# The up projection of a DiT layer: source order on all five engines, and the gated product through a PSUM bank

## The chip, the cores and the metric

The kernel runs on one core of a Trainium2 chip. The metric is the device time of one execution in microseconds (us). The kernel before took 873.97 us in the median of three runs (873.82, 873.97 and 875.6 us).

## The reference, cut to what matters

One layer of a diffusion transformer over 512 latent tokens of width 1024, in float32. A token mixer (retention and pooling) comes first; the part that the change touches is the second half, a gated MLP with a 3x3 depthwise convolution over the token grid (8 rows of 64) between the up projection and the activation:

```python
def _conv_ffn(u, rows, cols, w_up, conv_w, conv_b, w_down):
    h = (u @ w_up).reshape(B, rows, cols, 2 * D_FF)          # D_FF = 2816
    h = lax.conv_general_dilated(h, conv_w[:, :, None, :], (1, 1), 'SAME', ...) + conv_b
    a, b = jnp.split(h.reshape(B, L, 2 * D_FF), 2, axis=-1)
    return (jax.nn.gelu(a) * b) @ w_down
```

The result goes through a residual sum and a layer norm.

## The kernel before, in words

Every float32 product is three matmuls in the fp32r type. A helper (split, L86 to L91) casts an operand to a high part "hi" on ScalarE (ACT) and subtracts it from the operand on GpSimd (POOL) or VectorE (DVE), which gives the low part "lo" (the subtraction itself is L84). The helper mm3 (L94 to L96) then multiplies hi by hi, hi by lo and lo by hi into one PSUM bank.

The up stage is the loop over i at L1000. It takes 44 tiles of 128 features; tile i=2f is the "a" half and tile 2f+1 the "b" half of the gate pair f=0..21. Each tile is one PSUM bank of 128x512: 24 matmuls of 512 columns on TensorE (PE). For the first six tiles half of the columns are already done when the loop begins, and the loop does the other half. Then, for each tile:

- ACT writes the centre tap with the bias into an accumulator in SBUF (L1010) and two scaled copies (L1013);
- POOL adds these two copies, shifted, to the accumulator (L936), two taps;
- DVE does the other six taps (L938), each a multiply-add that reads the bank and the accumulator.

For an even tile ACT then applies gelu to the accumulator in place (gelu, L984). After the odd tile DVE multiplies the two accumulators (gated, L987). act_out makes the hi part of the product on ACT (L991) and the lo part on DVE (L84), both into the operand buffers of the down projection. up_prep(i) loads the weights of tile i (512 KB, issued on the SyncE queue, SP) and splits them: hi on ACT (L89, or L949 for every third tile), lo on POOL.

The down stage (L1044 on) multiplies the 22 products by w_down: 24 matmuls for each f, into eight banks that stay open. f=0, 1 and 2 are prepared by down_prep after the loop, f=3 (lo on DVE), f=4 (lo on POOL) and so on one ahead of their use. The layer norm at the end works on the finished banks.

What sets the order: `ordered(...)` names the engines whose instructions stay in the order of the source; the others are put in an order by a scheduler that goes by an estimate of when each instruction can start. In the up stage before, only SP keeps source order (`ORD3 = (E_SP,)`); PE, DVE, ACT and POOL are scheduled. Each engine then runs its own list strictly from the top, and an instruction that waits holds back those behind it on its engine.

Of the kernel before, what the change touches and what calls it, by code (L numbers as in the profile page):

```python
# [9 lines left out]
F32 = mybir.dt.float32  # L10
F32R = mybir.dt.float32r
AF = mybir.ActivationFunctionType
ALU = mybir.AluOpType

P = 128
D = 1024
# [4 lines left out]
NKT = D // P  # L21
NTB = SEQ // P
NFF = 2816 // P
# [9 lines left out]
E_PE, E_SP, E_DVE = mybir.EngineType.PE, mybir.EngineType.SP, mybir.EngineType.DVE  # L33
# [3 lines left out]
ORDS = (E_PE, E_SP, E_DVE, E_ACT, E_POOL)  # L37
# [1 line left out]
ORD1 = (E_SP,)  # L39
ORDB = (E_PE, E_SP)  # L40
ORD2 = (E_DVE, E_ACT, E_POOL)
ORD3 = (E_SP,)
ORDT = (E_SP,)


# [1 line left out]
def layer_kernel(ctx: ExitStack, tc: tile.TileContext, a: dict):  # L47
    nc = tc.nc
    act, dve, pool, pe, dma = nc.scalar, nc.vector, nc.gpsimd, nc.tensor, nc.sync
# [7 lines left out]
    def nm(s):  # L57
        count[0] += 1
        return f"{s}_{count[0]}"

    def slot(i, shape, dt=F32):
        return sb.tile(shape, dt, tag=f"S{i}", name=nm(f"S{i}"))

    def raw4(shape=(P, D)):
        return sb.tile(list(shape), F32, tag="raw", bufs=3, name=nm("raw"))
# [4 lines left out]
    def t2(shape=(P, SEQ), dt=F32):  # L70
        return sb.tile(list(shape), dt, tag="t2", bufs=8, name=nm("t2"))
# [8 lines left out]
    def bank():  # L80
        return ps_pool.tile([P, SEQ], F32, tag="ps", name=nm("ps"))

    def sub(eng, out, x, y):
        eng.tensor_tensor(out, x, y, ALU.subtract)  # L84

    def split(raw, shape, eng):  # L86
        hi = sb.tile(list(shape), F32R, tag="hi", bufs=2, name=nm("hi"))
        lo = sb.tile(list(shape), F32R, tag="lo", bufs=2, name=nm("lo"))
        act.copy(hi, raw)  # L89
        sub(eng, lo, raw, hi.bitcast(F32))  # L90
        return hi, lo  # L91
# [6 lines left out]
    def load(t, src):  # L98
        dma.dma_start(t, src)
        return t  # L100
# [41 lines left out]
    def alt():  # L142
        engs[0] += 1
        return dve if engs[0] % 2 else pool
# [6 lines left out]
    def ordered(*engines):  # L151
        if region[0] is not None:
            region[0].__exit__(None, None, None)
        region[0] = tc.manual_schedule(engines=set(engines)) if engines else None
        if engines:
            region[0].__enter__()
# [85 lines left out]
    def first_load(kt):  # L242
        for j in (kt, 8 + kt):
            load(ada_slot(j), a["wada"][j])
        return load(raw4((P, NF0)), a["w_first"][kt])
# [6 lines left out]
    def first_prep(kt, raw):  # L252
        w = split(raw, (P, NF0), pool)
        first_mod(kt)
        modulate(mod, kt, 8 + kt, xnT[:, kt, :], uh[:, kt, :], ul[:, kt, :], pool)
        return w
# [76 lines left out]
    ready = wh, wl  # L333
# [8 lines left out]
    for kt in range(NKT):  # L342
        wh, wl = ready
        if kt == 0:
# [7 lines left out]
            ready = split(first_load(1), (P, NF0), pool)  # L352
            first_mod(1)
            modulate(mod, 1, 9, xnT[:, 1, :], uh[:, 1, :], ul[:, 1, :], pool)
        elif kt + 1 < NKT:
            ready = first_prep(kt + 1, first_load(kt + 1))
# [534 lines left out]
    n_early = 6  # L891
# [27 lines left out]
    first_half(4)  # L919
    first_half(5)  # L920
    inner.__exit__(None, None, None)
    ordered(*ORD3)

    acts = [slot(s, [P, 8, SEQ], F32R) for s in (2, 7, 6, 5, 3, 0)]
    spare = [acts[i][:, 6:8, :].rearrange("p a b -> p (a b)") for i in (2, 5)]

    def grid(t):
        return t.rearrange("p (r c) -> p r c", r=ROWS)

    def tap(acc, src, w, dr, dc):  # L930
        r0, r1 = max(0, -dr), min(ROWS, ROWS - dr)
        c0, c1 = max(0, -dc), min(COLS, COLS - dc)
        o = grid(acc)[:, r0:r1, c0:c1]
        i = grid(src)[:, r0 + dr:r1 + dr, c0 + dc:c1 + dc]
        if w is None:
            pool.tensor_tensor(o, o, i, ALU.add)  # L936
        else:
            dve.scalar_tensor_tensor(o, i, w, o, ALU.mult, ALU.add)  # L938
# [3 lines left out]
    DVE_TAPS = (0, 2, 3, 5, 6, 8)  # L942
    prepped = {}
# [7 lines left out]
        return wh, wl  # L951

    def up_prep(i):
        if n_early <= i < 2 * NFF:
            raw = load(raw4((P, NKT, P)), a["w_up"][i])
            prepped[i] = (spare_split if i % 3 == 2 else split)(raw, (P, NKT, P), pool)

    def down_prep(f, eng):
        raw = load(raw4(), a["w_down"][f])
        return (split if f % 3 else spare_split)(raw, (P, D), eng)  # L960

    def up_mm(i):
        if i < n_early:
            half(i, 1)
            return early[i][0]
        wh, wl = prepped.pop(i)
        return feature_mm(wh, wl, NKT, u2h, u2l)

    srcs, accs = {}, {}

    def conv_taps(i, order):
        for n in order:
            tap(accs[i], srcs[i], convw[:, i, n:n + 1], *TAPS[n])
            yield

    def weave(*gens):
        gens = list(gens)
        while gens:
            for g in list(gens):
                if next(g, 0) == 0:  # L980
                    gens.remove(g)

    def gelu(f):
        act.activation(accs[2 * f], accs[2 * f], AF.Gelu_apprx_tanh)  # L984

    def gated(f):
        dve.tensor_tensor(accs[2 * f], accs[2 * f], accs[2 * f + 1], ALU.mult)  # L987

    def act_out(f):
        hi = acts[f // 8][:, f % 8, :]  # L990
        act.copy(hi, accs[2 * f])  # L991
        sub(dve, acts[3 + f // 8][:, f % 8, :], accs[2 * f], hi.bitcast(F32))

    def settle(i):
        if i >= 0 and i % 2 == 0:
            gelu(i // 2)
        elif i >= 0:
            gated(i // 2)

    for i in range(2 * NFF):  # L1000
        up_prep(i + 2)
        ps = up_mm(i)
        if i >= 2 * NFF - 2:
            src = t2()
            act.copy(src, ps)
        else:
            src = ps
        srcs[i] = src
        acc = accs[i] = t2()
        act.activation(acc, src, AF.Identity, bias=convb[:, i:i + 1], scale=convw[:, i, 4:5])  # L1010
        for n in POOL_TAPS:
            hs = t2()
            act.activation(hs, src, AF.Copy, scale=convw[:, i, n:n + 1])  # L1013
            tap(acc, hs, None, *TAPS[n])
        gens = [conv_taps(i, DVE_TAPS[:3])]
        if i:
            gens.insert(0, conv_taps(i - 1, DVE_TAPS[3:]))
        weave(*gens)
        settle(i - 1)
        if i >= 3 and i % 2 == 1:  # L1020
            act_out((i - 3) // 2)
    down0 = down_prep(0, pool)
    i = 2 * NFF - 1
    weave(conv_taps(i, DVE_TAPS[3:]))
    settle(i)
    act_out(NFF - 1)

    g2 = load(row(), gates[1:2, :].broadcast_to([P, D]))
    lng = load(row(), a["ln2_g"].broadcast_to([P, D]))
# [9 lines left out]
    def down(tb, f, wh, wl):  # L1039
        for hf, cs in enumerate(HALVES):  # L1040
            split_end = f == N_FRONT - 1 and hf == 1 and tb == NTB - 1
            down_mm(banks[tb][hf], tb, f, wh, wl, cs, f == 0, split_end)

    down1 = down_prep(1, dve)  # L1044
    for w, f in ((down0, 0), (down1, 1)):
        for tb in range(NTB - 1):
            down(tb, f, *w)
    ready = down_prep(2, pool)
    for w, f in ((down0, 0), (down1, 1)):
        down(NTB - 1, f, *w)  # L1050
    lasth = slot(1, [P, NFF - N_FRONT, D], F32R)
# [1 line left out]
    for f in range(2, N_FRONT):  # L1053
        w = ready
        if f + 1 < N_FRONT:
            ready = down_prep(f + 1, alt())
        for tb in range(NTB):
            down(tb, f, *w)
        if f >= N_FRONT - 8 and f % 2 == 0:
            i = (f - N_FRONT + 8) // 2  # L1060
            raw = load(raw4(), a["w_down"][N_FRONT + i])
# [143 lines left out]
```

## Time and profile before

| what | value |
|---|---|
| median of three runs | 873.97 us |
| the profiled execution | 874.79 us |
| its span, first to last instruction | 873.0 us |
| mean granted PE clock | 0.981 |
| busy: PE / DVE / ACT / POOL | 821.6 / 624.4 / 366.2 / 444.2 us |
| up stage (second halves of tiles 0 to 5, then 6 to 43) on PE | from about 500 to 726 us |

The busy times are sums over the whole span; the stretch from 500 to 760 us is the one to read here. In the rows below, a timeline row gives the start, the time from the first start to the last end, the engine, the line, the operation, the operands by name (t an accumulator or a scaled copy, ps a PSUM bank, S an operand buffer, hi and lo the parts of a weight, raw a loaded weight), and how many instructions it joins. The time in brackets is idle time ahead of the row and what ended it.

### The profile page before, as it was taken

The numbers are of one execution on the slowest core, as the hardware profiler recorded it, in microseconds if no ns is written. First come the engines' busy times: TensorE is split into PE (matmuls) and PEld (weight loads), VectorE is DVE, ScalarE is ACT, GpSimd is POOL, SyncE is SP. The second block draws the span as 40 slices with busy tenths as digits, with TensorE's granted clock in tenths as the row PEclk, the third lists the DMA queues.
The fourth block names the chain that finished last, engine by engine and source line by source line (L and its number), as shares of the span: only waits on it lengthen the run. The fifth ranks groups of instructions, "written<-read, shape, count | busy, mean of one in ns | idle before, by whom it ended". The sixth has DMA issues, their size and how long they took to land.

```text
span 873.0 us, 10556 instructions
## 1 busy us (share of the span) xinstructions
PE 821.6 (94%) x3865; PEld 678.5 (78%) x3865; DVE 624.4 (72%) x959; ACT 366.2 (42%) x575; POOL 444.2 (51%) x304
## 2 busy tenths in 40 slices
PE   6889989999999999998998899999999998799993
PEld 4667878778888888887787898888888776688883
DVE  7899996676267773346757769999999999612138
ACT  4434544121444343233335476666655565223200
POOL 4877411121543230113456878899888886212245
PEclk9999999999999999999999999999999999999997
DMA  9932466767221104344503312222222252224202
GB/s 352 345 105 94 127 207 218 236 226 216 72 73 49 50 1 145 100 154 163 196 1 121 121 50 84 86 96 99 96 97 95 75 169 83 87 97 144 73 1 96
DMA packets 33780, 106.94 MB, mean 122 GB/s; under 512 B 4528, under 2 KB 5312, under 8 KB 33728
## 3 DMA queue, kind: packets, MB, share of 16 engines
q1 hardware_dynamic: 33728, 106.27, 35.6%
q8 instruction: 30, 0.49, 0.2%
q14 instruction: 22, 0.18, 0.1%
HBM read 104.14 MB, written 2.11 MB: 122 GB/s over the span
## 4 chain that ended last, share of the span: by engine, by line
PE 40%; DVE 39%; POOL 8%; DMA 6%; issue 5%; ACT 2%; SPq 0%; DVEq 0%; POOLq 0%; ACTq 0%
DVE t L938 19%; PE ps L96 11%; PE ps L95 11%; PE ps L94 11%; DVE S L84 4%; DMA raw<-in_wada 4%; DVE t L987 3%; POOL lo L84 3%; DVE raw L203 2%; DVE lo L84 2%; PE ps L339 1%; POOL S L84 1%; POOL sm L123 1%; PE ps L608 1%; DVE sm L130 1%
## 5 line engine op out<-in xcount | busy, mean ns | idle before, releaser
L96 PE MATMUL ps<-S,lo 128*128 128x512 f32 (+1 forms) x544 | 212.2, 392 | 5.1 <-DVE lo L84 4.7
L94 PE MATMUL ps<-S,hi 128*128 128x512 f32 (+1 forms) x544 | 213.6, 393 | 2.7 <-ACT hi L89 2.7
L95 PE MATMUL ps<-S,hi 128*128 128x512 f32 (+1 forms) x544 | 212.5, 391 | 0.2 <-POOL S L84 0.2
L84 POOL TENSOR_TENSOR lo<-raw,hi 128x1024 fp32r<-128x1024 f32 (+1 forms) x53 | 134.0, 2530 | 107.2 <-ACT hi L89 105.3
L938 DVE SCALAR_TENSOR_TENSOR t<-ps,convw,t 128x441 f32<-128x441 f32 (+1 forms) x252 | 167.6, 693 | 15.8 <-POOL t L936 11.5
L89 ACT CAST hi<-raw 128x1024 fp32r<-128x1024 f32 (+1 forms) x98 | 98.9, 1009 | 168.2 <-PE ps L95 61.7
L96 PEld LDWEIGHTS ps<-S,lo 128*128 128x128 f32 x544 | 102.8, 189 | 29.8 <-DVE lo L84 6.8
L94 PEld LDWEIGHTS ps<-S,hi 128*128 128x128 f32 x544 | 103.6, 190 | 23.7 <-ACT hi L89 3.1
L936 POOL TENSOR_TENSOR t<-t,t 128x448 f32<-128x448 f32 x88 | 116.7, 1329 | 10.0 <-ACT t L1013 6.2
L95 PEld LDWEIGHTS ps<-S,hi 128*128 128x128 f32 x544 | 103.7, 191 | 21.3 <-POOL S L84 0.6
L95 PE MATMUL ps<-S,S 128*128 128x512 f32 (+1 forms) x308 | 113.8, 370 | 5.4 <-DVE S L84 5.0
L94 PE MATMUL ps<-S,S 128*128 128x512 f32 (+1 forms) x308 | 113.1, 369 | 3.6 <-DVE t L938 3.6
L96 PE MATMUL ps<-S,S 128*128 128x512 f32 (+1 forms) x308 | 113.8, 370 | 0.2 <-POOL S L84 0.2
L84 DVE TENSOR_TENSOR lo<-raw,hi 128x1024 fp32r<-128x1024 f32 (+1 forms) x47 | 61.4, 1307 | 53.0 <-ACT hi L89 53.0
L84 POOL TENSOR_TENSOR S<-raw,S 128x1024 fp32r<-128x1024 f32 x21 | 50.8, 2423 | 68.7 <-ACT S L735 44.5
L95 PE MATMUL ps<-lo,S 128*128 128x512 f32 x208 | 81.6, 392 | 0.7 <-DVE lo L84 0.6
L96 PE MATMUL ps<-hi,S 128*128 128x512 f32 x208 | 81.3, 391 | 0.0
L94 PE MATMUL ps<-hi,S 128*128 128x512 f32 x208 | 79.2, 392 | 0.0
L95 PEld LDWEIGHTS ps<-S,S 128*128 128x128 f32 x308 | 58.9, 191 | 15.6 <-DVE S L84 5.5
L94 PEld LDWEIGHTS ps<-S,S 128*128 128x128 f32 x308 | 58.6, 191 | 13.6 <-DVE t L938 4.0
L96 PEld LDWEIGHTS ps<-S,S 128*128 128x128 f32 x308 | 58.9, 191 | 10.4 <-POOL S L84 1.1
L84 POOL TENSOR_TENSOR S<-t,S 128x512 fp32r<-128x512 f32 (+1 forms) x29 | 44.8, 1557 | 31.2 <-DVE t L220 11.1
(205 smaller groups left out, 1187.3 us busy)
## 6 DMA issues: line engine op xcount, KB each, us to landing
raw<-in_w_up SPq DMA_DIRECT2D x44, 512.0 KB, 3.3
raw<-in_wada SPq DMA_DIRECT2D x32, 512.0 KB, 4.2
raw<-in_w_down SPq DMA_DIRECT2D x22, 512.0 KB, 3.3
S<-in_wada SPq DMA_DIRECT2D x16, 512.0 KB, 6.8
raw<-in_w_first SPq DMA_DIRECT2D x8, 512.0 KB, 7.4
raw<-in_w_v SPq DMA_DIRECT2D x16, 256.0 KB, 3.3
raw<-in_w_ga SPq DMA_DIRECT2D x8, 512.0 KB, 3.4
raw<-in_w_gb SPq DMA_DIRECT2D x8, 512.0 KB, 3.3
```

Source lines behind the costliest of these rows:

```text
L84: eng.tensor_tensor(out, x, y, ALU.subtract)
L89: act.copy(hi, raw)
L94: pe.matmul(out, lhsT=sh, rhs=mh, start=first, stop=False)
L95: pe.matmul(out, lhsT=sh, rhs=ml, start=False, stop=False)
L96: pe.matmul(out, lhsT=sl, rhs=mh, start=False, stop=last)
L123: pool.tensor_scalar(rs, mv[:, 1:2], EPS, None, ALU.add)
L130: dve.bn_stats(st[:, hf, :], src[:, hf * SEQ:(hf + 1) * SEQ])
L203: dve.scalar_tensor_tensor(out_junk, raw, 1.0, silu_c, ALU.mult, ALU.mult, accum_out=mod[:, j:j + 1])
L339: pe.matmul(g0[f], lhsT=w[:, f * P:(f + 1) * P], rhs=m[:, kt, :], start=kt == 0 and i == 0, stop=kt == NKT - 1 and i == 2)
L936: pool.tensor_tensor(o, o, i, ALU.add)
L938: dve.scalar_tensor_tensor(o, i, w, o, ALU.mult, ALU.add)
L987: dve.tensor_tensor(accs[2 * f], accs[2 * f], accs[2 * f + 1], ALU.mult)
```

## The change

All five engines keep source order in the up stage, and only SP from the down stage on. The gelu writes into a fresh PSUM bank (for the last two pairs into an SBUF tile), the product is formed there in place, and both parts of act_out read it there. The loop's source is rearranged: weights are prepared three tiles ahead, including w_down for f=0, 1, 2 as "tiles" 44 to 46 (lo on POOL; for f=1 it was DVE), tiles 6, 7 and 8 at i=0, 2 and 4. In an odd iteration i=2f+1 the product parts of pair f-1 and then the gelu of pair f follow the taps. Only the last tile's bank is copied to SBUF first (it was the last two).

```diff
-ORD3 = (E_SP,)
...
-    ordered(*ORD3)
+    ordered(*ORDS)
...
     def up_prep(i):
-        if n_early <= i < 2 * NFF:
+        if i < 2 * NFF:
             raw = load(raw4((P, NKT, P)), a["w_up"][i])
-            prepped[i] = (spare_split if i % 3 == 2 else split)(raw, (P, NKT, P), pool)
+            shape = (P, NKT, P)
+        else:
+            raw = load(raw4(), a["w_down"][i - 2 * NFF])
+            shape = (P, D)
+        prepped[i] = (spare_split if i % 3 == 2 else split)(raw, shape, pool)
...
+    prod = {}
+    AHEAD = 3
     def gelu(f):
-        act.activation(accs[2 * f], accs[2 * f], AF.Gelu_apprx_tanh)
+        prod[f] = bank() if f < NFF - 2 else t2()
+        act.activation(prod[f], accs[2 * f], AF.Gelu_apprx_tanh)
 
     def gated(f):
-        dve.tensor_tensor(accs[2 * f], accs[2 * f], accs[2 * f + 1], ALU.mult)
+        dve.tensor_tensor(prod[f], prod[f], accs[2 * f + 1], ALU.mult)
-    def act_out(f):
+    def act_out_hi(f):
+        act.copy(acts[f // 8][:, f % 8, :], prod[f])
+    def act_out_lo(f):
         hi = acts[f // 8][:, f % 8, :]
-        act.copy(hi, accs[2 * f])
-        sub(dve, acts[3 + f // 8][:, f % 8, :], accs[2 * f], hi.bitcast(F32))
+        sub(dve, acts[3 + f // 8][:, f % 8, :], prod[f], hi.bitcast(F32))
...
     for i in range(2 * NFF):
-        up_prep(i + 2)
+        if i in (0, 2, 4):
+            up_prep(n_early + i // 2)
         ps = up_mm(i)
-        if i >= 2 * NFF - 2:
+        if i == 2 * NFF - 1:
             src = t2()
             act.copy(src, ps)
...
+        if i >= n_early:
+            up_prep(i + AHEAD)
         gens = [conv_taps(i, DVE_TAPS[:3])]
         if i:
             gens.insert(0, conv_taps(i - 1, DVE_TAPS[3:]))
         weave(*gens)
-        settle(i - 1)
-        if i >= 3 and i % 2 == 1:
-            act_out((i - 3) // 2)
-    down0 = down_prep(0, pool)
-    i = 2 * NFF - 1
-    weave(conv_taps(i, DVE_TAPS[3:]))
-    settle(i)
-    act_out(NFF - 1)
+        f, odd = divmod(i - 1, 2)
+        if i and odd:
+            gated(f)
+        elif i:
+            if f:
+                act_out_hi(f - 1)
+                act_out_lo(f - 1)
+            gelu(f)
+    down0, down1, down2 = (prepped.pop(2 * NFF + f) for f in range(3))
+    weave(conv_taps(2 * NFF - 1, DVE_TAPS[3:]))
+    gated(NFF - 1)
+    act_out_hi(NFF - 1)
+    act_out_lo(NFF - 1)
+    ordered(E_SP)
```

In the lists that follow a name carries a number; a row is the line, the operation, output<-inputs.

**ACT, about gate pair 4.** Before (tiles 8 to 12 have the accumulators t2_654, t2_659, t2_666, t2_673 and t2_678):

```order
L984 ACTIVATE t2_640_4283<-t2_640_4283 128x512
L949 CAST S6_610_4004<-raw_676_4532 128x1024
L1010 ACTIVATE t2_673_4515<-ps_672_4490,convb_3401,convw_3399 128x512
L1013 ACTIVATE t2_674_4517<-ps_672_4490,convw_3399 128x512
L1013 ACTIVATE t2_675_4520<-ps_672_4490,convw_3399 128x512
L991 CAST S2_608_4002<-t2_640_4283 128x512
L984 ACTIVATE t2_654_4377<-t2_654_4377 128x512
L89 CAST hi_682_4578<-raw_681_4576 128x1024
L1010 ACTIVATE t2_678_4561<-ps_677_4536,convb_3401,convw_3399 128x512
L1013 ACTIVATE t2_679_4563<-ps_677_4536,convw_3399 128x512
```

In the changed kernel (tiles 8, 9 and 10 have t2_658, t2_663 and t2_671; the cast is L88, the tap's parts L1016 and L1019, the gelu L993, the product's hi part L999):

```order
L1016 ACTIVATE t2_663_4425<-ps_662_4400,convb_3401,convw_3399 128x512
L1019 ACTIVATE t2_664_4427<-ps_662_4400,convw_3399 128x512
L1019 ACTIVATE t2_665_4430<-ps_662_4400,convw_3399 128x512
L88 CAST hi_667_4435<-raw_666_4433 128x1024
L999 CAST S2_608_4002<-ps_656_4354 128x512
L993 ACTIVATE ps_669_4447<-t2_658_4381 128x512
L1016 ACTIVATE t2_671_4474<-ps_670_4449,convb_3401,convw_3399 128x512
L1019 ACTIVATE t2_672_4476<-ps_670_4449,convw_3399 128x512
```

The gelu of tile 8 stood behind the centre tap and the copies of tile 11, and ahead of those of tile 12; now it stands ahead of those of tile 10.

**POOL, the same place, in the changed kernel** (tile 10 and tile 11, whose accumulator is t2_678; the weights that are split, L83, are those of tiles 12 and 13):

```order
L83 TENSOR_TENSOR lo_668_4436<-raw_666_4433,hi_667_4435 128x1024
L935 TENSOR_TENSOR t2_671_4474<-t2_671_4474,t2_672_4476 128x448
L935 TENSOR_TENSOR t2_671_4474<-t2_671_4474,t2_673_4479 128x448
L83 TENSOR_TENSOR lo_676_4485<-raw_674_4482,hi_675_4484 128x1024
L935 TENSOR_TENSOR t2_678_4520<-t2_678_4520,t2_679_4522 128x448
```

The pattern of two taps and one split for each tile is that of before; the split is of tile i+3 now, where it was of tile i+2.

**DVE, the same place.** Before:

```order
L987 TENSOR_TENSOR t2_640_4283<-t2_640_4283,t2_647_4329 128x512
L938 SCALAR_TENSOR_TENSOR t2_654_4377<-ps_653_4352,convw_3399,t2_654_4377 128x7x63
L938 SCALAR_TENSOR_TENSOR t2_659_4421<-ps_658_4396,convw_3399,t2_659_4421 128x8x63
L938 SCALAR_TENSOR_TENSOR t2_666_4469<-ps_665_4444,convw_3399,t2_666_4469 128x7x63
L938 SCALAR_TENSOR_TENSOR t2_654_4377<-ps_653_4352,convw_3399,t2_654_4377 128x7x63
L938 SCALAR_TENSOR_TENSOR t2_659_4421<-ps_658_4396,convw_3399,t2_659_4421 128x8x63
L938 SCALAR_TENSOR_TENSOR t2_666_4469<-ps_665_4444,convw_3399,t2_666_4469 128x7x63
L84 TENSOR_TENSOR S5_611_4005<-t2_640_4283,S2_608_4002 128x512
```

In the changed kernel (taps L937, product L996, lo part L83):

```order
L996 TENSOR_TENSOR ps_669_4447<-ps_669_4447,t2_663_4425 128x512
L937 SCALAR_TENSOR_TENSOR t2_671_4474<-ps_670_4449,convw_3399,t2_671_4474 128x8x63
L937 SCALAR_TENSOR_TENSOR t2_678_4520<-ps_677_4495,convw_3399,t2_678_4520 128x7x63
L937 SCALAR_TENSOR_TENSOR t2_671_4474<-ps_670_4449,convw_3399,t2_671_4474 128x7x63
L937 SCALAR_TENSOR_TENSOR t2_678_4520<-ps_677_4495,convw_3399,t2_678_4520 128x7x63
L937 SCALAR_TENSOR_TENSOR t2_671_4474<-ps_670_4449,convw_3399,t2_671_4474 128x7x63
L937 SCALAR_TENSOR_TENSOR t2_678_4520<-ps_677_4495,convw_3399,t2_678_4520 128x8x63
L83 TENSOR_TENSOR S5_611_4005<-ps_669_4447,S2_608_4002 128x512
```

The taps of two neighbouring tiles alternate strictly; before, those of up to three tiles were mixed. The last tap of the even tile 10 now stands behind the first tap of the odd tile 11.

**SP.** In the changed kernel three loads of 512 KB (the g2, ln2_g and ln2_b rows of the last stage) stand between the loads of w_up 4 and w_up 6; before they stood behind that of w_down 0.

## Rows read from the trace of the kernel before

**Rows 1.** The page: its first line, and the busy time of DVE.

```profile
span 873.0 us, 10556 instructions
PE 821.6 (94%) x3865; PEld 678.5 (78%) x3865; DVE 624.4 (72%) x959; ACT 366.2 (42%) x575; POOL 444.2 (51%) x304
```

**Rows 2.** Windows: busy us (instructions) of PE, PEld, DVE, ACT, POOL, granted clock, DMA share, GB/s.

```profile
600.00:650.00 50.00, 50.00 (x222) 41.45 (x221) 48.23 (x60) 29.94 (x45) 43.72 (x27) 1.00 0.28 95
```

**Rows 3.** Chain of waits from 500 to 780 us, shares by line.

```profile
by line: DVE t L938 59.0%; DVE S L84 11.4%; DVE t L987 9.7%; issue 5.6%; PE ps L95 3.6%; PE ps L96 3.3%; PE ps L94 3.0%; POOL t L936 1.9%; POOL lo L84 1.5%; POOL S L84 0.6%; DVE lo L84 0.4%; ACT hi L89 0.4%; DVEq L987 0.1%; POOLq L84 0.0%; 
```

**Rows 4.** Timeline of DVE, two gate products in the middle of the up stage.

```profile
645.32 1.36 DVE L987 TENSOR_TENSOR t<-t,t 128x512 f32<-128x512 f32 x1
646.60 2.94 DVE L938 SCALAR_TENSOR_TENSOR t<-ps,convw,t 128x441 f32<-128x441 f32 x4
649.45 1.87 DVE L84 TENSOR_TENSOR S<-t,S 128x512 fp32r<-128x512 f32 x1
651.24 5.66 DVE L938 SCALAR_TENSOR_TENSOR t<-ps,convw,t 128x441 f32<-128x441 f32 x8
657.00 1.37 DVE L987 TENSOR_TENSOR t<-t,t 128x512 f32<-128x512 f32 x1
```

**Rows 5.** Timeline of PE: two matmuls of one run, the first down products, the last wait.

```profile
639.63 0.39 PE L96 MATMUL ps<-S,lo 128*128 128x512 f32 x1
...
641.67 0.39 PE L96 MATMUL ps<-S,lo 128*128 128x512 f32 x1
...
726.87 0.50 PE L95 MATMUL ps<-S,S 128*128 128x512 f32 x1 [0.37 <-POOL S L84]
...
754.50 0.80 PE L95 MATMUL ps<-S,S 128*128 128x512 f32 x1 [5.04 <-DVE S L84]
```

**Rows 6.** Timeline of DVE at other places: PSUM operands, and SBUF operands alone.

```profile
477.99 0.67 DVE L818 TENSOR_TENSOR S<-ps,row 128x512 f32<-128x512 f32 x1
...
510.21 13.54 DVE L938 SCALAR_TENSOR_TENSOR t<-ps,convw,t 128x441 f32<-128x441 f32 x22 [11.06 <-POOL t L936]
...
738.43 2.13 DVE L938 SCALAR_TENSOR_TENSOR t<-t,convw,t 128x441 f32<-128x441 f32 x1
...
753.23 1.22 DVE L84 TENSOR_TENSOR S<-raw,S 128x1024 fp32r<-128x1024 f32 x1
754.37 0.68 DVE L987 TENSOR_TENSOR t<-t,t 128x512 f32<-128x512 f32 x1
```

**Rows 7.** Timeline of POOL: taps and splits alone, and taps beside two-SBUF work of DVE.

```profile
506.78 11.59 POOL L936 TENSOR_TENSOR t<-t,t 128x448 f32<-128x448 f32 x10
...
644.97 2.73 POOL L936 TENSOR_TENSOR t<-t,t 128x448 f32<-128x448 f32 x2
...
735.34 2.38 POOL L936 TENSOR_TENSOR t<-t,t 128x448 f32<-128x448 f32 x2 [5.86 <-ACT t L1013]
737.67 2.41 POOL L84 TENSOR_TENSOR lo<-raw,hi 128x1024 fp32r<-128x1024 f32 x1
```

**Rows 8.** Timeline of ACT: tile 1, the gelu's table, one steady tile, and before a POOL tap.

```profile
506.21 0.78 ACT L1010 ACTIVATE t<-ps,convb,convw 128x512 f32<-128x512 f32 x1
...
519.19 1.28 ACT L984 ACT_TABLE_LOAD   x1
...
640.97 0.63 ACT L984 ACTIVATE t<-t 128x512 f32<-128x512 f32 x1 [2.54 <-DVE t L938]
641.50 1.03 ACT L89 CAST hi<-raw 128x1024 fp32r<-128x1024 f32 x1
642.44 0.77 ACT L1010 ACTIVATE t<-ps,convb,convw 128x512 f32<-128x512 f32 x1
643.11 1.26 ACT L1013 ACTIVATE t<-ps,convw 128x512 f32<-128x512 f32 x2
...
734.56 1.32 ACT L1013 ACTIVATE t<-t,convw 128x512 f32<-128x512 f32 x2
```

**Rows 9.** Timeline of SP's DMA queue: the load of w_up 6.

```profile
485.82 0.33 SPq L99 DMA_DIRECT2D raw<-in_w_up  x1
```

More of the change, by code (lines that the diff above doesn't have):

```diff
@@ L981, in weave @@
                     gens.remove(g)
+    prod = {}
+    AHEAD = 3
     def gelu(f):
-        act.activation(accs[2 * f], accs[2 * f], AF.Gelu_apprx_tanh)
+        prod[f] = bank() if f < NFF - 2 else t2()
+        act.activation(prod[f], accs[2 * f], AF.Gelu_apprx_tanh)
     def gated(f):
-        dve.tensor_tensor(accs[2 * f], accs[2 * f], accs[2 * f + 1], ALU.mult)
-    def act_out(f):
+        dve.tensor_tensor(prod[f], prod[f], accs[2 * f + 1], ALU.mult)
+    def act_out_hi(f):
+        act.copy(acts[f // 8][:, f % 8, :], prod[f])
+    def act_out_lo(f):
         hi = acts[f // 8][:, f % 8, :]
-        act.copy(hi, accs[2 * f])
-        sub(dve, acts[3 + f // 8][:, f % 8, :], accs[2 * f], hi.bitcast(F32))
[L994 to L998, printed above, removed]
+        sub(dve, acts[3 + f // 8][:, f % 8, :], prod[f], hi.bitcast(F32))
     for i in range(2 * NFF):
-        up_prep(i + 2)
+        if i in (0, 2, 4):
+            up_prep(n_early + i // 2)
         ps = up_mm(i)
-        if i >= 2 * NFF - 2:
+        if i == 2 * NFF - 1:
             src = t2()
@@ L1042, in down @@
             down_mm(banks[tb][hf], tb, f, wh, wl, cs, f == 0, split_end)
-    down1 = down_prep(1, dve)
     for w, f in ((down0, 0), (down1, 1)):
@@ L1047, in layer_kernel @@
             down(tb, f, *w)
-    ready = down_prep(2, pool)
+    ready = down2
     for w, f in ((down0, 0), (down1, 1)):
```

## The prediction

> **What bounds the kernel now.** I read the windows first: from 600 to 650 us PE is busy all the time at full granted clock, DVE for 48.23 of 50 us, POOL for 43.72 [rows 2]. One matmul follows another by (641.67 - 639.63) / 9 = 0.2267 us [rows 5], so a tile of 24 costs 5.44 and a pair of tiles 10.88 us: PE runs back to back through the up stage, and the down products begin at 726.87 [rows 5]. So the up stage is already at PE's pace, although DVE carries most of the chain of waits (59% for the taps, 11% and 10% for the gated product and its low part) [rows 3]. What the kernel loses there comes at its end. DVE needs 11.68 us for a pair (from one product at 645.32 to the next at 657.00 [rows 4]) against PE's 10.88, falls behind, and pays when PE has run out of tiles: the 72 down matmuls of f=0 to 2 would take 72 x 0.2267 = 16.3 us, to 743.2, but f=3 goes on only at 754.50, after its low part from DVE [rows 5, 6]. These 11.3 us are all that a faster DVE can win here; the share of 72% of the page [rows 1] doesn't tell this.
>
> **What gets cheaper.** The product takes 1.36 and its low part 1.87 us in the loop [rows 4], with two SBUF operands beside a busy POOL; without POOL a product takes 0.68 [rows 6]. With one operand in PSUM a tensor_tensor of 128x512 took 0.67 [rows 6]; the row that writes PSUM from DVE doesn't exist, so I bound the new product by 0.60 (0.67 less the overlap of successive starts) and 1.36, and take 0.60, as the nearest row has the same operands and only another target. Per pair DVE drops by (1.28 + 1.79) - 2 x 0.60 = 1.9 us. Taps of different tiles also overlap better: 22 of them took 13.54, 0.615 each [rows 6], against 5.66 / 8 = 0.71 in the loop [rows 4]. New DVE work: 12 x 0.615 + 1.2 = 8.6 us a pair, below PE. [...]
>
> **What gets dearer: a closed chain.** The order lists show it. The gelu of pair f waits for the last tap of even tile e=2f, and behind it on ACT now stands the centre tap of tile e+2, where before three more tiles were through. Before, ACT stood idle 2.54 us ahead of each gelu and it cost nothing [rows 8]. Now the next pair hangs on it, in this order of steps, from the last tap of e to that of e+2:
>
> - DVE to ACT 0.05 (an estimate: the gaps between such rows are 0.03 to 0.08); gelu 0.53 (640.97 to 641.50), centre tap 0.67 (642.44 to 643.11) [rows 8]. ACT writing PSUM has no row: bounds 0.45 and 0.63 for the gelu, 0.53 taken since the input is the same;
> - POOL's first tap starts 0.78 after the first copy does (734.56 to 735.34 [rows 7, 8]); with a bank as source the copies take 1.26 and not 1.32 for two, so 0.75;
> - on POOL two taps 2.33 (735.34 to 737.67), the split for tile e+5 2.36 (2.41 less the overlap), the two taps of the odd tile e+3 2.38 [rows 7];
> - 0.03 to DVE, where the first tap of e+3 stands ahead of the last two of e+2: 3 x 0.615 + 0.69 = 2.54.
>
> The sum is 11.64 us a pair: more than PE's 10.88, and more than DVE's own way round (taps of both tiles, product, 11.2). ACT's and DVE's other work lies beside it. The Trainium skill (PSUM — Partial Sum Buffer, "Engine vs sequencer instructions") calls the ACT, DVE and GpSimd queues strict FIFO: by that the gelu really blocks the taps behind it, which is the sum taken here; were it to let them pass, the time would be the second rival's.
>
> **Head.** Tile 1's centre tap starts at 506.21 [rows 8]; with 0.67, 0.75, 2.38 and 2.57 the last tap of tile 0 ends at 512.6. The gelu's table load (1.28) lay in spare time before [rows 8]; now it stands behind the wait. Then gelu 0.53, the cast for tile 7 0.94, its split on POOL 0.08 + 2.36, POOL's taps of tile 2 2.38, and on DVE five taps, a product, and the last taps of tile 2 (3.08 + 0.60 + 0.62 + 1.85 + 0.69, with 0.08 of gaps): 14.5 us to tile 2 (527.1), and without the table 13.2 to tile 4 (540.3). Tile 9's low part is ready 6.7 us later, at 547.0; PE, done with tile 8 by about 537 (its low part comes at 531), idles 10 us there. From tile 4 to tile 40 are 18 pairs: 540.3 + 18 x 11.64 = **749.8 = T**.
>
> **Tail.** Gelu, centre tap, copy: POOL starts tile 42's taps at T+2.0, then the split of w_down 1 (T+4.3), tile 43's taps (T+6.7), the split of w_down 2 (T+9.1 to 11.4); these splits are the moved down preparation. Tile 43 is read from SBUF, so its first tap has two SBUF operands and meets that last split: such a tap took 2.13 and ended 0.5 after the split did (738.43 + 2.13 = 740.56 against 740.08 [rows 6, 7]). It ends at T+11.9, and three more taps give tile 42's last at T+13.9. Then a tap 0.62, a low part 0.60, three taps of tile 43 one after the other 2.16, product 0.68, its cast 0.58, the cast of w_down 3 1.04, its low part on DVE 0.08 + 1.22 [rows 6]: 6.98, so f=3 has its low part at T+20.9 = 770.7, where before it had it at 754.45. **The sum: +16.2 us.** From there the down stage has the same order and work in both, so the difference stays.
>
> Edits with one answer: the three row loads on SP now stand ahead of w_up 5 and w_up 6. They wait for DVE to free their buffers, by 486.9, and w_up 6 went out at 485.82 [rows 9]; with 1 MB more on the queues it lands perhaps 4 us later, hidden since tile 6 comes after six half tiles on PE. Without that cover it would be 4 us once. The lo of w_down 1 leaves DVE and is in the walk above; one bank copy fewer on ACT is worth 0.58 in the tail, beside POOL. The banks that the products take are returned a pair later, and PE is then only some 1.3 tiles ahead: it waits, but ACT's centre tap still finds its bank ready.
>
> **The forecast.** The profiled execution has 874.8 us, 0.8 above the median of 873.97; against that median 873.97 + 16.2 = **890** us. The gelu's bounds move 18 pairs by -1.4 to +1.8, handoffs of 0.03 to 0.08 in three places by 3 either way, and a granted clock that doesn't fall after the last wait may return one: its own range is 884 to 896.
>
> **Rivals.**
> - The chain is under 10.88, by shorter handoffs and a faster gelu into PSUM; it needs 0.76 off. PE then sets the pace from tile 9 on: 540.3 + 18 x 10.88 = 736.1, f=3 at 757.0, +2.5: **876.5** (874 to 879). The head's loss stays. For it: each term is one row's. Against: POOL's 7.1 us of it can hardly shrink.
> - The relief comes through whole (the other side): ACT runs ahead of its gelu's wait after all, or the first pairs don't wait for the splits of tiles 7 and 8, so that products follow at 10.88 or less from the first pair on. PE keeps its pace to 726, DVE with 2.3 us to spare in each pair isn't late at the end, and the 11.3 us go: 873.97 - 11.3 = **863** (859 to 868). For it: rows 2 to 6. Against: the order on ACT.
> - POOL's taps stay at 2.73 a pair, as in the loop before [rows 7], because in the new order other DVE work still blocks it, or the product in PSUM costs 1.36: two pairs of taps at 0.4 more give 12.4 a pair, 18 x 0.8 = 14 more: **904** (898 to 908). This is also the case in which the change doesn't do what it says. Against: ten taps took 1.16 each while 22 DVE taps with a bank operand ran beside them [rows 6, 7].
>
> **How the numbers follow.** Forecast 0.70, PE's pace 0.13, whole relief 0.10, blocked POOL 0.07. The likeliest has 890. From 874 to 899 lie the forecast, nearly all of the first rival and a little of the third: 0.8. Faster by over 0.2% (about what a measurement here can tell from no change, 1.7 us): the second rival and 0.05 for an error in the head and tail of the first two, 0.15. Within 0.2%: the low end of the first, 0.05. Slower: 0.80.
>
> **What would show it.** Right: gelu starts (L993) 11.6 apart from 560 to 740; ACT's gelu waiting for DVE taps, and right behind it POOL waiting for ACT; POOL busy without a gap from a tap pair to the next but idle about 2 us a pair; a product at 0.67; a PE gap near 540 of some 10 us; f=3 near 770. Wrong: PE full from 560 to 720 (second rival), gelu starts 10.88 apart (first), or tap pairs on POOL over 2.6 (third).

## The result, and the profile after

The changed kernel took **886.87 us** in the median of four runs (885.02 to 888.75) against 874.3 us of the kernel before beside it (873.82 to 875.6): a ratio of 1.0145, 95% interval 1.0121 to 1.0169. So it is slower by 12.6 us; the forecast was 890, with its likeliest case between 884 and 896. The profiled execution took 885.02 us, the shortest of the four; its span is 882.8 us against 873.0.

The view of waits in the changed kernel, 490 to 775 us (engine, line, who was waited for: us in total, times, longest), names the loop that the prediction summed:

```profile
DVE t L937 <- POOL t L935: 75.5, 41, 8.3
ACT ps L993 <- DVE t L937: 54.6, 19, 2.9
POOL t L935 <- ACT t L1019: 50.3, 21, 6.4
```

DVE waits for POOL's taps, ACT's gelu for DVE's last tap, and POOL for ACT's scaled copies that stand behind the gelu. None of these three costs much alone; together they are a circle, one waiting for the next. One turn of it is seen in the timelines of ACT, POOL and DVE:

```profile
641.11 0.60 ACT L993 ACTIVATE ps<-t 128x512 f32<-128x512 f32 x1 [2.93 <-DVE t L937]
641.65 0.76 ACT L1016 ACTIVATE t<-ps,convb,convw 128x512 f32<-128x512 f32 x1
642.31 1.26 ACT L1019 ACTIVATE t<-ps,convw 128x512 f32<-128x512 f32 x2
...
652.73 0.60 ACT L993 ACTIVATE ps<-t 128x512 f32<-128x512 f32 x1 [2.92 <-DVE t L937]
```

```profile
643.07 2.39 POOL L935 TENSOR_TENSOR t<-t,t 128x448 f32<-128x448 f32 x2 [2.15 <-ACT t L1019]
645.42 2.40 POOL L83 TENSOR_TENSOR lo<-raw,hi 128x1024 fp32r<-128x1024 f32 x1
647.78 2.39 POOL L935 TENSOR_TENSOR t<-t,t 128x448 f32<-128x448 f32 x2
650.13 2.41 POOL L83 TENSOR_TENSOR lo<-raw,hi 128x1024 fp32r<-128x1024 f32 x1
```

```profile
648.49 0.69 DVE L996 TENSOR_TENSOR ps<-ps,t 128x512 f32<-128x512 f32 x1
649.09 0.73 DVE L937 SCALAR_TENSOR_TENSOR t<-ps,convw,t 128x504 f32<-128x504 f32 x1
650.20 3.08 DVE L937 SCALAR_TENSOR_TENSOR t<-ps,convw,t 128x441 f32<-128x441 f32 x5 [0.38 <-POOL t L935]
653.20 0.68 DVE L83 TENSOR_TENSOR S<-ps,S 128x512 fp32r<-128x512 f32 x1
```

From gelu to gelu 11.62 us pass. Read it as a walk: gelu at 641.11, centre tap 641.65, copies 642.31, POOL 643.07 to 650.13 without a gap (taps, split, taps), DVE from 650.20, the even tile's last tap as the fifth of six, gelu at 652.73. Beside [rows 4], the product fell from 1.36 to 0.69 us and its low part from 1.87 to 0.68: DVE got its relief, and now stands idle for 12 of the 50 us shown below.

The windows of PE say the same (busy us and count of PE, PEld, DVE, ACT, POOL, then the granted clock, DMA share and GB/s):

```profile
500.00:560.00 60.00, 50.45 (x257) 42.67 (x257) 39.44 (x64) 30.30 (x46) 36.91 (x26) 0.89 0.13 45
...
600.00:650.00 50.00, 47.87 (x206) 38.02 (x205) 37.95 (x62) 28.43 (x42) 40.73 (x27) 1.00 0.27 91
```

From 600 to 650 us PE issued 206 matmuls where it issued 222 [rows 2], and DVE was busy 38 of 50 us where it was 48: neither is the bound now. The chain of waits from 500 to 780 us moved accordingly: POOL's taps have 24% of it, DVE's taps 19%, and "issue", time in which an engine waits for nothing shown, 25%; before, DVE's taps had 59% [rows 3].

**Where the time went.** Not all of the difference of the two profiled spans, 9.8 us, is the change's. The first bank copy of the first stages, in code that the change leaves alone, stands in the timelines of DVE at 219.38 before and 215.64 after:

```profile
219.38 0.69 DVE L578 COPY S<-ps 128x512 f32<-128x512 f32 x1 [2.81 <-PE ps L96]
```

```profile
215.64 0.69 DVE L577 COPY S<-ps 128x512 f32<-128x512 f32 x1 [2.48 <-PE ps L95]
```

This execution was 3.7 us early before the up stage began. Without that the span would differ by 13.5 us, which is nearer to the 12.6 of the medians. (In the nine profiled executions the first centre tap started anywhere from 499.8 to 504.3 us; to compare profiled executions I take the time from that tap to the end of the span: 368.7 us before, 383.0 after.)

### The profile page after: what moved, and what is told of

Same layout as the page of the kernel before. It is cut to its first block, busy times and chain, and to the rows that moved or that the text cites. A ratio compares the mean times of both kernels' runs of the same rounds, so it can differ in the third digit from the quotient of the medians.

```text
span 882.8 us, 10505 instructions
## 1 busy us (share of the span) xinstructions
PE 822.8 (93%) x3865; PEld 676.6 (77%) x3865; DVE 580.8 (66%) x958; ACT 363.8 (41%) x574; POOL 429.0 (49%) x305
## 4 chain that ended last, share of the span: by engine, by line
PE 41%; DVE 19%; POOL 16%; issue 12%; ACT 6%; DMA 5%; POOLq 0%; SPq 0%; DVEq 0%; ACTq 0%
PE ps L95 12%; PE ps L94 11%; PE ps L93 11%; POOL t L935 8%; DVE t L937 6%; POOL lo L83 4%; DMA raw<-in_wada 4%; DVE lo L83 2%; DVE raw L202 2%; POOL S L83 2%; ACT t L1016 2%; PE ps L338 1%; ACT t L1019 1%; ACT ps L993 1%; POOL sm L122 1%
## 5 line engine op out<-in xcount | busy, mean ns | idle before, releaser
L937 DVE SCALAR_TENSOR_TENSOR t<-ps,convw,t 128x441 f32<-128x441 f32 (+1 forms) x258 | 164.0, 690 | 75.2 <-POOL t L935 75.1
L94 PE MATMUL ps<-S,hi 128*128 128x512 f32 (+1 forms) x544 | 212.1, 390 | 0.0
L83 POOL TENSOR_TENSOR lo<-raw,hi 128x1024 fp32r<-128x1024 f32 (+1 forms) x54 | 134.0, 2481 | 98.2 <-ACT hi L88 96.1
L88 ACT CAST hi<-raw 128x1024 fp32r<-128x1024 f32 (+1 forms) x98 | 99.4, 1015 | 159.1 <-PE ps L94 49.4
L935 POOL TENSOR_TENSOR t<-t,t 128x448 f32<-128x448 f32 x88 | 101.8, 1158 | 53.7 <-ACT t L1019 50.3
L94 PEld LDWEIGHTS ps<-S,hi 128*128 128x128 f32 x544 | 103.4, 190 | 20.9
L94 PE MATMUL ps<-S,S 128*128 128x512 f32 (+1 forms) x308 | 112.9, 366 | 0.0
L83 DVE TENSOR_TENSOR lo<-raw,hi 128x1024 fp32r<-128x1024 f32 (+1 forms) x46 | 61.6, 1339 | 50.2 <-ACT hi L88 50.0
L94 PE MATMUL ps<-lo,S 128*128 128x512 f32 x208 | 81.1, 390 | 0.8 <-POOL lo L83 0.8
L83 POOL TENSOR_TENSOR S<-raw,S 128x1024 fp32r<-128x1024 f32 x21 | 50.9, 2424 | 62.6 <-ACT S L734 44.4
L95 PE MATMUL ps<-hi,S 128*128 128x512 f32 x208 | 81.0, 389 | 0.0
L93 PE MATMUL ps<-hi,S 128*128 128x512 f32 x208 | 77.5, 391 | 0.0
L94 PEld LDWEIGHTS ps<-S,S 128*128 128x128 f32 x308 | 58.9, 191 | 9.3
L83 POOL TENSOR_TENSOR S<-t,S 128x512 fp32r<-128x512 f32 (+1 forms) x29 | 45.0, 1566 | 30.7 <-DVE t L219 11.1
```

Of the source, the lines that this page charges most:

```text
L93: pe.matmul(out, lhsT=sh, rhs=mh, start=first, stop=False)
L94: pe.matmul(out, lhsT=sh, rhs=ml, start=False, stop=False)
L95: pe.matmul(out, lhsT=sl, rhs=mh, start=False, stop=last)
```

## The experiments

The theory was the prediction's: a closed chain through ACT's gelu. The rivals: the order of POOL and DVE costs by itself; the product in PSUM takes a bank that PE wants; PE or the head decides. The kernel before, run beside them, took 872.77 us (runs 1, 2, 4 and 5) and 873.8 us (runs 3, 6 and 7); each ratio is to that.

**1. The gelu moved back on ACT.** One edit to the changed kernel:

```diff
         if i >= n_early:
             up_prep(i + AHEAD)
+        if i >= 2 and i % 2 == 0:
+            gelu(i // 2 - 1)
         gens = [conv_taps(i, DVE_TAPS[:3])]
...
                 act_out_lo(f - 1)
-            gelu(f)
...
+    gelu(NFF - 1)
     weave(conv_taps(2 * NFF - 1, DVE_TAPS[3:]))
```

> The changed kernel with one thing moved: the gelu of pair f stands on ACT behind the centre tap, the copies and the weight cast of tile 2f+2, no longer ahead of them. Theory (the closed chain of 11.6 us a pair through ACT's gelu bounds the changed kernel): the shortest way round is now gelu, centre tap of the odd tile, its POOL taps and three DVE taps, 0.05 + 0.53 + 0.67 + 0.75 + 2.38 + 0.03 + 2.54 = 6.95 us, below the 10.88 of PE, so PE runs back to back, the head's 10 us gap goes too, and the end of the up stage is early: 861 us (857 to 866), gelu starts 10.88 apart. Rival (the strict order of POOL and DVE, or the product in PSUM, is what costs, and not where the gelu stands): 883 to 890 us, as the changed kernel.

Measured: **858.88 us**, ratio to the kernel before 0.9848 (0.9812 to 0.9884): faster than both kernels. The windows of its PE, with the columns as above:

```profile
600.00:650.00 50.00, 50.00 (x223) 41.39 (x222) 39.90 (x65) 31.41 (x47) 43.17 (x29) 1.00 0.29 100
...
700.00:750.00 50.00, 50.00 (x223) 41.39 (x222) 34.18 (x48) 22.83 (x32) 30.77 (x19) 1.00 0.28 96
```

From 540 to 800 us PE is never idle, through the end of the up stage and into the down stage, where the kernel before lost 11.3 us [rows 5], and gelu starts are 10.88 us apart, as the theory has it. ACT now waits for PE, and not for DVE, and the gelu follows the weight cast with no gap:

```profile
641.87 0.78 ACT L1016 ACTIVATE t<-ps,convb,convw 128x512 f32<-128x512 f32 x1 [2.14 <-PE ps L95]
...
643.68 1.06 ACT L88 CAST hi<-raw 128x1024 fp32r<-128x1024 f32 x1
644.62 0.62 ACT L993 ACTIVATE ps<-t 128x512 f32<-128x512 f32 x1
```

The rival that laid the loss on POOL's and DVE's order falls: both orders, and the bank, are unchanged here. The place of one instruction in each pair was worth about 27 us: 12.6 above the kernel before beside 13.9 below it, and 383.0 against 355.8 us from the first centre tap to the end.

**2. The split behind the odd tile's taps.**

```diff
-        if i >= n_early:
+        if i > n_early and i % 2:
+            up_prep(i + AHEAD - 1)
             up_prep(i + AHEAD)
```

> The changed kernel, gelu where it was, but the weight splits of an even and an odd iteration both come in the odd one, so on POOL the split (2.36 us) no longer stands between the taps of the even and those of the odd tile. Theory: the chain through POOL falls by 2.36 to 9.28 us, and the next longest way round decides, that of DVE (both tiles' taps and the product after the even tile's POOL taps), 11.2 us: 18 pairs gain 0.4 each, 7 to 8 us, so 879 us (877 to 882), gelu starts 11.2 apart. Rival (POOL's split is not on the chain): no change from 887, gelu starts 11.6 apart. Second rival (PE's pace is the next bound and DVE's way is shorter than summed): 10.9 apart, 874.

Measured: 889.17 us, ratio 1.0180 (1.0149 to 1.0212), gelu starts still 11.61 apart. The theory's number missed; the timelines of ACT and POOL say why:

```profile
642.58 0.60 ACT L993 ACTIVATE ps<-t 128x512 f32<-128x512 f32 x1 [2.10 <-DVE t L937]
...
647.80 0.78 ACT L1016 ACTIVATE t<-ps,convb,convw 128x512 f32<-128x512 f32 x1 [2.75 <-PE ps L95]
...
659.41 0.78 ACT L1016 ACTIVATE t<-ps,convb,convw 128x512 f32<-128x512 f32 x1 [2.77 <-PE ps L95]
```

```profile
649.24 2.40 POOL L935 TENSOR_TENSOR t<-t,t 128x448 f32<-128x448 f32 x2 [2.16 <-ACT t L1019]
651.59 4.78 POOL L83 TENSOR_TENSOR lo<-raw,hi 128x1024 fp32r<-128x1024 f32 x2
```

The odd tile's centre tap now waits for PE. The edit closed another circle: odd centre tap at 647.80, its taps on POOL to 651.59, the first split to about 653.95, then PE's tile with those weights, 5.44, which gives 659.4: the next odd centre tap starts at 659.41. It happened to be as long as the first. So this run said nothing on the split's place in the first circle, since two things had been moved in it: the split out of the chain, and the weights of an odd tile (those that the even iteration prepares) to a later time.

**3. The split moved the other way,** ahead of the gelu, into the 2.15 us in which POOL waits for it. (The weights are again those that the even iteration prepares, three tiles on, so an odd tile's; the expectation calls them an even tile's.)

```diff
-        ps = up_mm(i)
+        ps = pss.pop(i) if i in pss else up_mm(i)
...
-        if i >= n_early:
-            up_prep(i + AHEAD)
+        if i >= n_early - 1 and i % 2:
+            if i > n_early:
+                up_prep(i + AHEAD)
+            if i + 1 < 2 * NFF:
+                pss[i + 1] = up_mm(i + 1)
+                up_prep(i + 1 + AHEAD)
```

> The changed kernel, gelu and product where they were, but the weights of an even tile are cast and split one iteration earlier (still three tiles ahead of what PE has been given), so that POOL does that split while it waits for the gelu and not between the taps of the even and the odd tile. No other split comes later than before. Theory (the closed chain runs through POOL's split): without its 2.36 us the chain is 9.28 us, the next way round is that of DVE, 11.2 us, and a pair takes 11.2 instead of 11.6: 879 us (877 to 882). Rival (the split never mattered, as the earlier run with the split behind the odd taps seems to say): 11.6 a pair, 887 us. Third (PE's pace decides): 10.9 a pair, 874 us.

Measured: 876.9 us, ratio 1.0034 (1.0019 to 1.0048). The gelu starts are 11.14 us apart (ACT), and POOL does both tiles' taps in one piece:

```profile
641.12 0.60 ACT L994 ACTIVATE ps<-t 128x512 f32<-128x512 f32 x1 [2.45 <-DVE t L937]
...
652.26 0.60 ACT L994 ACTIVATE ps<-t 128x512 f32<-128x512 f32 x1 [2.45 <-DVE t L937]
```

```profile
643.07 4.76 POOL L935 TENSOR_TENSOR t<-t,t 128x448 f32<-128x448 f32 x4 [1.66 <-ACT t L1020]
```

So the split was on the chain, and with it gone the next way round, DVE's 11.2, decides as summed. The time is 0.1 below the range given: to the gelu of pair 19 the run is 8.0 us ahead, as forecast (17 pairs of 0.48), and 1.5 us come behind it, in the tail.

**4. The order without the PSUM bank.**

```diff
-        prod[f] = bank() if f < NFF - 2 else t2()
+        prod[f] = accs[2 * f]
```

> The changed kernel's order, but gelu and product stay in the SBUF accumulator as in the kernel before. Theory: the order makes the loss, and the PSUM product only keeps DVE and POOL out of each other's way; with two SBUF operands the product costs 1.4 and the low part up to 1.9 us again and POOL's taps are held up for part of that, so a pair takes 12.0 to 12.4 us and the kernel 894 to 901 us. Rival (the PSUM bank itself is what costs, since the product holds a bank that PE wants): faster than the changed kernel, 870 to 880 us. If the bank makes no difference: 887.

Measured: 893.73 us, ratio 1.0238 (1.0207 to 1.0269), 0.3 below the theory's range. Rows of DVE and POOL:

```profile
652.07 0.98 DVE L996 TENSOR_TENSOR t<-t,t 128x512 f32<-128x512 f32 x1
```

```profile
651.35 2.72 POOL L935 TENSOR_TENSOR t<-t,t 128x448 f32<-128x448 f32 x2
```

The product with two SBUF operands takes 0.98 us and POOL's odd taps, which it meets, 2.72 and not 2.39. That 0.33 is on the chain: gelu starts are 11.95 apart, 0.33 more than in the changed kernel, and 18 to 20 pairs of it are 5.9 to 6.6 us. The medians differ by 6.9, and the stretches from the first centre tap to the end by 7.6; the rest is not accounted for. So in this order the bank is worth about 7 us, by POOL's taps and not by DVE's own time.

**5. The PSUM bank without the order.** The kernel before, with gelu's output, product and act_out on `prod[f] = bank()` for f < 20.

> The kernel before with its scheduled order, but gelu writes the product into a PSUM bank (the first 20 pairs), as in the change. Theory: DVE's product and low part fall to 0.6 each, 1.9 us a pair, DVE is no longer late when PE has run out of tiles, and up to the 11.3 us that PE waits there go: 863 to 867 us. Rival (the bank is taken from PE, which had all eight): PE waits for banks in the loop and the time is 873 or more.

Measured: **963.84 us**, ratio 1.1046 (1.1006 to 1.1085). The theory missed by 100 us, and the rival named the sign but not the cause. ACT's timeline:

```profile
640.27 0.60 ACT L987 ACTIVATE ps<-t 128x512 f32<-128x512 f32 x1 [4.66 <-DVE t L938]
645.72 0.58 ACT L994 CAST S<-ps 128x512 fp32r<-128x512 f32 x1 [4.85 <-DVE ps L990]
...
647.15 0.79 ACT L1013 ACTIVATE t<-ps,convb,convw 128x512 f32<-128x512 f32 x1
...
656.50 0.60 ACT L987 ACTIVATE ps<-t 128x512 f32<-128x512 f32 x1 [4.65 <-DVE t L938]
```

The scheduler now puts the product's high part right behind its own gelu on ACT, so ACT waits twice in each pair, 4.7 us for the gelu and 4.9 for the product, with the next tiles' centre taps behind both. A pair takes 16.23 us. PE's repeated waits are for weights (20.9 us for ACT's hi part and 18.2 for POOL's low part, 11 times each from 490 to 850 us), not for banks. DVE's list changed too (the six taps of a tile now follow one another), and no run puts ACT's order back alone: that it is ACT's order that costs is read from the waits. That the scheduler does this in order to give the bank back soon is my reading, not shown.

**6. The late gelu without the PSUM bank:** the edits of 1 and 4 together.

> The run with the gelu behind the next even tile's work on ACT, but gelu and product stay in the SBUF accumulator: the order without the PSUM bank. Theory (order alone decides, and DVE has room): DVE needs 12 x 0.615 + 1.0 to 1.4 for the product + 0.7 to 1.9 for the low part = 9.1 to 10.7 us a pair, still under PE's 10.88, POOL 9.5 to 10.3; PE stays back to back and the time is that of the run with the bank, 859 us (857 to 862). Rival (the PSUM product carries the gain, since DVE's two-SBUF operations and POOL's hold each other up): 866 to 874 us.

Measured: 863.76 us, ratio 0.9881 (0.9856 to 0.9905): 1.8 above the theory's range and 2.2 below the rival's, so the time alone decides for neither. PE (first numbers) and DVE of one window, a product, and PE's wait in the head, of this run and then of run 1:

```profile
600.00:650.00 50.00, 50.00 (x222) 41.42 (x221) 46.41 (x65) 32.11 (x47) 46.15 (x29) 1.00 0.29 101
```

```profile
643.25 1.40 DVE L996 TENSOR_TENSOR t<-t,t 128x512 f32<-128x512 f32 x1
```

```profile
536.58 0.50 PE L95 MATMUL ps<-S,lo 128*128 128x512 f32 x1 [2.16 <-POOL lo L83]
```

```profile
533.12 0.50 PE L95 MATMUL ps<-S,lo 128*128 128x512 f32 x1 [0.95 <-POOL lo L83]
```

In the loop PE is as full as in run 1, and from 600 us on gelu starts are 10.88 us apart in both, though the product costs 1.40 again and DVE is busy 46.4 of 50 us. From the first centre tap to the end it takes 358.6 us where run 1 takes 355.8, and these 2.8 us lie in the head. PE's wait there is 1.2 us longer, and behind it eight matmuls take 3.38 us (537.64 to 541.02), where at 0.2267 they take 1.81: 1.6 us more. The granted clock is 0.88 from 530 to 540 us and 0.95 from 540 to 550; in run 1 it is 1.00 in both. So of the gain over the kernel before, 14 us with the bank, 10 come from the order alone; the bank adds 3 to 4 (each time against the kernel before beside it), in the head and not in the loop, and room on DVE.

**7. The head.** Tiles 6, 7 and 8 prepared at i=0.

```diff
-        if i in (0, 2, 4):
-            up_prep(n_early + i // 2)
+        if i == 0:
+            for k in range(3):
+                up_prep(n_early + k)
```

> The changed kernel with the weights of tiles 6, 7 and 8 all cast and split ahead of the loop's first tile, not at i=0, 2 and 4. Theory (in the head the cast 0.94 and the split 2.44 of tiles 7 and 8 stand between a gelu and the next taps): from the centre tap of tile 0 to the gelu of pair 2 the changed kernel took 36.9 us; without the two steps two pairs are 2.0 us shorter each (then DVE's own way round decides), so 33 us, less up to 1 us if the splits delay the first taps on POOL; the kernel takes 883 us (881 to 886). Rival (the head is PE's or DVE's own and the splits lie beside it): 36 to 37 us, 887.

Measured: 885.97 us, ratio 1.0139 (1.0117 to 1.0161): at the top of the theory's range, but no difference that can be told from the changed kernel (1.0145) either. Its ACT:

```profile
501.99 1.05 ACT L88 CAST hi<-raw 128x1024 fp32r<-128x1024 f32 x1 [7.30 <-PE ps L94]
...
515.62 1.28 ACT L993 ACT_TABLE_LOAD   x1 [7.98 <-DVE t L937]
516.92 0.60 ACT L993 ACTIVATE ps<-t 128x512 f32<-128x512 f32 x1
...
528.00 0.60 ACT L993 ACTIVATE ps<-t 128x512 f32<-128x512 f32 x1 [2.45 <-DVE t L937]
...
539.14 0.60 ACT L993 ACTIVATE ps<-t 128x512 f32<-128x512 f32 x1 [2.45 <-DVE t L937]
```

The first three gelus are 11.1 us apart, where they were 13.1 and 13.2: 2.0 us less each, as the theory has it. But the cast of tile 7 had to wait for PE until 501.99, the splits moved ahead of tile 0's taps on POOL, and the first gelu came 13.0 us after the first centre tap and not 10.6. Of the 4.1 us won 2.5 were given back there: 35.2 from the first centre tap to the gelu of pair 2, between the theory's 33 to 34 and the rival's 36 to 37. The first centre tap itself stands behind the casts of tiles 7 and 8 here (501.99 to 503.89), which a count from that tap leaves out.

## Why the prediction was right, point by point

Shown means: in the profile of the changed kernel or by a run.

- **DVE's relief is real** (0.69 and 0.68 for 1.36 and 1.87), as taken. As time on DVE it was worth nothing in this order, since DVE was no longer the bound; what the bank gave here is the 0.33 us a pair on POOL's taps that run 4 lost. Worked out 8.6 us a pair; DVE was busy 38.0 of 50 us, or 8.8 for each 11.6.
- **The chain of 11.64** is 11.62, and each term fits within 0.1. Its members were shown by taking them out: the gelu's place by run 1 (10.88, PE's pace), the split by run 3 (11.14, the next way round, which the text gave as 11.2), POOL's taps by run 4 (0.33 longer, and the pair by as much).
- **The head.** Forecast 14.5 and 13.2 us from the last tap of tile 0 to that of tile 2 and on to tile 4. In the timeline of ACT the table load starts at 509.07, where the last tap of tile 0 has ended, and the next two gelus at 523.49 and 536.67: 14.4 and 13.2. The table load (1.28) was indeed behind the wait:

```profile
499.80 0.78 ACT L1016 ACTIVATE t<-ps,convb,convw 128x512 f32<-128x512 f32 x1 [6.60 <-PE ps L95]
...
509.07 1.28 ACT L993 ACT_TABLE_LOAD   x1 [4.44 <-DVE t L937]
510.37 0.60 ACT L993 ACTIVATE ps<-t 128x512 f32<-128x512 f32 x1
...
523.49 0.60 ACT L993 ACTIVATE ps<-t 128x512 f32<-128x512 f32 x1 [2.46 <-DVE t L937]
...
536.67 0.60 ACT L993 ACTIVATE ps<-t 128x512 f32<-128x512 f32 x1 [2.45 <-DVE t L937]
```

- **PE's gap** was forecast as one of 10 us before tile 9. It came in pieces: 5.2 us ahead of 519.31, for a bank that DVE's taps held (the wait names the taps; the bank is my reading), and 1.9 and 2.4 at 540 and 543 for the weights of tile 9. The first I had not seen. It cost nothing, since PE was not on the chain.
- **The tail.** The gelu of pair 20 starts at 745.61, that of pair 21 at 759.67 (14.1 us, forecast 13.9), and the low part of f=3 is done at 765.34 + 1.23 = 766.57, 21.0 after T (forecast 20.9). The tap of tile 43 that meets the split took 2.80 us:

```profile
755.02 2.80 DVE L937 SCALAR_TENSOR_TENSOR t<-t,convw,t 128x441 f32<-128x441 f32 x1 [0.39 <-POOL t L935]
...
765.34 1.23 DVE L83 TENSOR_TENSOR S<-raw,S 128x1024 fp32r<-128x1024 f32 x1 [0.25 <-ACT S L948]
```

- **The loads on SP.** For "perhaps 4 us" the text gave no row. The cast of tile 6, which waits for its load in both kernels, started at 488.97 before and at 488.29 after, or 492.0 with the 3.7 us of the early start added: 3 us later. It was hidden, as forecast.
- **The step that was mis-sized** is the last of the sum: "From there the down stage has the same order and work in both, so the difference stays." The low part came 12.1 us later than before, 15.9 with the 3.7 us added: the 16.2 was right within 0.3 up to there. But what PE still had to do behind it was not the same. Before, and then in the changed kernel (the rows with ps<-hi,S are the first of f=4):

```profile
757.66 0.41 PE L94 MATMUL ps<-S,S 128*128 128x512 f32 x1
...
761.10 0.39 PE L94 MATMUL ps<-hi,S 128*128 128x512 f32 x1
```

```profile
765.36 2.12 PE L93 MATMUL ps<-S,S 128*128 128x512 f32 x8 [1.11 <-ACT S L948]
...
770.95 0.39 PE L93 MATMUL ps<-hi,S 128*128 128x512 f32 x1
```

Before, PE stood idle for 5.04 us [rows 5] with two of the 24 products of f=3 done (two of L94 from 748.73). The first seven of the 22 that were left took 3.16 us, from 754.50 to 757.66, and not 7 x 0.2267 = 1.59; the granted clock was 0.55 from 754.4 to 758. So f=4 began 6.6 us after the low part. In the changed kernel PE waited 1.11 us, did the eight products that need no low part first, and went on at a granted clock of 1.00: f=4 began 4.4 us after the low part (766.57 to 770.95). I had compared the low parts and not what PE still had to do after them, and had the clock's return ("may return one") in the range but not in the sum: together 2.3 us too much, 1.6 of them the slow matmuls. That leaves 13.6, which the starts of f=4 give directly (770.95 - 761.10 + 3.7); the medians differ by 12.6, and the rest is within what single executions vary by (885.02 to 888.75 us).
- **The rivals.** POOL's taps took 2.39 a pair, so the third was wrong for this kernel; run 4 shows the 2.7 that it meant, in the order without the bank. The second, the whole relief at 859 to 868, is what run 1 has at 858.88: it failed by the order on ACT alone. Run 1 even won more than the 11.3 us that the text called all that could be won: 12.9 from the first centre tap to the end, which fits 11.3 and the 1.6 us of slow matmuls behind the wait that is gone. The first, PE's pace from tile 9 on, wasn't reached.

The prediction's sentence from the Trainium skill (PSUM — Partial Sum Buffer, "Engine vs sequencer instructions") on strict FIFO queues fits these runs: run 1 differs from the changed kernel in the place of the gelu in ACT's queue alone, and the 2.9 us for which ACT waited for DVE ahead of each gelu, with the next tile's taps behind it, are gone. That a product with two SBUF operands and POOL's taps hold each other up is run 4 against the changed kernel: 0.98 and 2.72 us against 0.69 and 2.39.

## What to carry to other kernels

As run 1 shows, an instruction that waits on a slow engine belongs, in an in-order queue, behind the work that this engine will need next: follow one pair from a wait back to the same wait, over all engines, add up, and compare the sum with the bound engine's pace. The wait view gives such a circle away: its largest waits recur once or twice a pair (41, 19 and 21 times here), and their names close on each other. And an edit that shortens one circle can close another of the same length, so look at which wait took its place before saying that a step didn't matter.

## What the runs showed that I had not expected

- Freeing DVE by a PSUM bank, alone, cost 91 us: the scheduler then ordered ACT's list otherwise, and ACT waited twice in each pair (run 5). The same bank under a written order with the late gelu gained 14.
- Executions differ by some 4 us before the up stage, in code that is the same in all of them: the first bank copy started between 215.6 and 219.8 us in the nine profiled executions, and the first centre tap between 499.8 and 504.3. A difference of two spans of that size says nothing until the start of the stage has been compared.
- Moving preparation ahead of the loop moved a wait too: the cast of run 7 waited 7.30 us for PE, by its operands for a buffer that PE still read.
